# A tree-attention kernel: each iteration's Q/K transposes move ahead of its score matmuls, and the K copy moves ahead of its exponentials

## The chip, the cores and the metric

One NeuronCore of a Trainium2 chip runs the whole program. The metric is the device time in microseconds of one execution. Five executions of the kernel before were timed, and one further execution was taken by the hardware profiler; the profile's own span runs from the program's first to its last instruction, and the execution's time is a little longer than that span.

## The reference

Attention over 8 batches of 12 heads, 512 positions and 64 dimensions, where position i sees only itself and its ancestors in a binary tree (parent of i is (i-1)//2):

```python
mask = np.zeros((seq, seq))
for i in range(seq):
    mask[i, i] = 1
    parent = i
    while parent > 0:
        parent = (parent - 1) // 2
        mask[i, parent] = 1
scores = np.einsum('bhqd,bhkd->bhqk', Q, K) * scale
scores = scores + (1 - mask) * (-1e9)
weights = np.exp(scores - np.max(scores, axis=-1, keepdims=True))
weights = weights / (np.sum(weights, axis=-1, keepdims=True) + 1e-10)
return np.einsum('bhqk,bhkd->bhqd', weights, V).astype(np.float32)
```

## The kernel before

The unit of work is a pair of heads: 8 batches of 6 pairs make 48 pairs, numbered 0 to 47. Since a position has few ancestors, a pair doesn't compute the full 512x512 score matrix. It scores every query against one tile of 128 keys near the root (`st1`, two heads of 128x512) and against four further tiles of 128 keys, each for 96 queries (`stx`, two heads of 128x384). The mask is put into PSUM by a matmul of constant codes (`ctile`) before the matmul of K and Q adds the scores.

A pair passes through three functions.

- `transposes(i)` (line 267): 16 TensorE transposes, 8 of Q into the PSUM tile `tq` and 8 of K into `tk`; then VectorE copies `tq` to the SBUF tile `qt` (line 297), and ScalarE copies `tk` to `kt` (line 298).
- `scores(i)` (line 304): TensorE writes the codes and then K times Q into `st` (one copy in PSUM), ScalarE takes the exponential into `et` (line 324); then TensorE does the same for `stx` (one copy), and ScalarE takes the exponential into `etx` (line 335).
- `values(i)` (line 342): 48 TensorE matmuls of `et` and `etx` with V and a column of ones into `o` (one copy in PSUM); VectorE takes the reciprocal of the sums (line 364) and multiplies (line 367); SyncE issues the output DMA of 256 KB (line 371).

`tq`, `tk`, `st`, `stx` and `o` stand in PSUM pools with one buffer each, so the next pair's writer waits until the last pair's reader is done. `qt` and `kt` have four buffers, `et` and `etx` three.

The inputs come in by DMAs that GpSimd issues (line 222), which turn fp32 into bf16 on the way. A hand-written plan sets their order. For a batch b between 1 and 6 it is: Q and K of heads 0 to 3, Q and K of heads 4 to 7, V of batch b+1, Q and K of heads 8 to 11. GpSimd does nothing else and runs ahead of the compute. V has to be spread into two layouts by VectorE: `copies(spread(...))` (line 261) gives ten copies for each batch, two in each of the iterations of pairs 1 to 5 of the batch before. The last batch has no such copies, since no V is left.

The whole program runs under a manual schedule, so that each engine executes its instructions in program order. The loop is a software pipeline:

```python
for i in range(N):
    b, hp = pairs[i]
    load(i + 9)
    if i + 1 < N:
        scores(i + 1)
    if i + 2 < N:
        transposes(i + 2)
    values(i)
```

TensorE's order in iteration i is therefore scores of i+1, transposes of i+2, values of i. ScalarE's order is exponential of `st` and of `stx` of pair i+1, then the K copy of pair i+2. VectorE's order is the Q copy of i+2, the reciprocal and the product of i, then the V copies.

Of the kernel before, what the change touches and what calls it, by code (L numbers as in the profile page):

```python
# [126 lines left out]
def kernel(  # L127
# [88 lines left out]
    def load(upto):  # L216
        while plan and plan[-1][0] <= upto:
            _, src, b, h0, h1 = plan.pop()
            kind = "q" if src is Q else "k" if src is K else "v"
            if (kind, b) not in loaded:  # L220
                loaded[kind, b] = stage.tile([P, H, T * D], bf16, name=kind + "s")
            nc.gpsimd.dma_start(  # L222
                out=loaded[kind, b][:, h0:h1, :],
                in_=src[b, h0:h1].rearrange("h (p t) d -> p h (t d)", t=T),
            )
# [6 lines left out]
    def spread(b, h0, h1):  # L232
        vs = loaded["v", b]
        v1, vx = v1s[b % NV], vxs[b % NV]
        v = vs[:, h0:h1, :].rearrange("p h (t d) -> p h t d", t=T)
        big = [
            (vx[64:P, h0:h1, 0:3:2, 0:D], v[64:P, :, 0:3:2, :]),
            (vx[0:64, h0:h1, 1:4:2, 0:D], v[64:P, :, 1:4:2, :]),
        ]
        for part, c, t0, t1 in ((0, 0, 1, 2), (32, 0, 3, 0), (64, 1, 2, 1),  # L240
                                (96, 1, 0, 3)):
            assert KORD[XW[c] + part // 32] == (t0, 1)
            assert KORD[XW[c + 2] + part // 32] == (t1, 1)
            big.append((
                vx[part:part + 32, h0:h1, c:c + 3:2, 0:D],
                pick(v[32:64], t0, t1),
            ))
        small = [
            (v1[32 * r:32 * r + 32, h0:h1, 0:D], v[0:32, :, KORD[K1 + r][0], :])
            for r in range(T)  # L250
        ]
        ops = []
        for n in range(6):
            ops.append(big[n])
            if n % 3:
                ops.append(small.pop())
        return ops

    def copies(ops):
        for o, i in ops:  # L260
            nc.vector.tensor_copy(out=o, in_=i)  # L261

    pairs = [(b, hp) for b in range(B) for hp in range(HP)]
    N = len(pairs)
    state = {}

    def transposes(i):
        b, hp = pairs[i]
        qs, ks = loaded["q", b], loaded["k", b]
        tq = psumT.tile([P, 512], bf16)  # L270
        tk = psumT.tile([P, 576], bf16)

        def put(o, src, t, mat):
            for hi in range(2):
                nc.tensor.matmul(  # L275
                    out=o[D * hi:D * hi + D], rhs=perms[mat],
                    lhsT=src[:, 2 * hp + hi, D * t:D * t + D],
                    start=True, stop=True, is_transpose=True,
                )

        put(tq[:, 64:192], qs, 0, 1)
        put(tq[:, 0:384].rearrange("d (c x) -> d c x", c=2)[:, :, 0:64], qs, 1, 0)
        for t in range(2, T):
            put(tq[:, P * t:P * t + P], qs, t, 0)
        for t in range(T):
            at = kput[t][1]
            if at[1] - at[0] == 32:
                step, run = at[2] - at[0], 64
            else:
                step, run = at[1] - at[0], 32  # L290
                assert at[2] - at[1] == step
            o = tk[:, at[0]:]
            o = bass.AP(o.tensor, o.offset, [list(o.ap[0]), [step, P // run], [1, run]])
            put(o, ks, t, 2 + t)
        qt = work.tile([P, 512], bf16)
        kt = work.tile([P, 512], bf16)
        nc.vector.tensor_copy(out=qt[:, :], in_=tq[:, :])  # L297
        nc.scalar.copy(  # L298
            out=kt[:, :].rearrange("d (i j x) -> d i j x", j=2, x=32),
            in_=tk[:, :].rearrange("d (j i x) -> d i j x", j=2, x=32)[:, 0:8],  # L300
        )
        state[i] = (qt, kt)

    def scores(i):
        b, hp = pairs[i]
        q_, k_ = state[i]
        st1 = psumS.tile([P, 2, 512], fp32)
        stx = psumS.tile([P, 2, 512], fp32)

        def mm(dst, lhsT, rhs, first):  # L310
            nc.tensor.matmul(  # L311
                out=dst, lhsT=lhsT, rhs=rhs, start=first, stop=True,
                skip_group_check=not first,
            )

        hb = [slice(D * hi, D * hi + D) for hi in range(2)]
        q = [q_[hb[hi], :] for hi in range(2)]
        k = [k_[hb[hi], :] for hi in range(2)]
        for hi in range(2):
            mm(st1[:, hi, :], ck1[hb[hi], :], cq1[hb[hi], :], True)  # L320
        for hi in range(2):
            mm(st1[:, hi, :], k[hi][:, 32 * K1:32 * K1 + P], q[hi], False)
        et1 = et1pool.tile([P, 2, 512], bf16)
        nc.scalar.activation(  # L324
            out=et1[:, :, :], in_=st1[:, :, :], func=AF.Exp, scale=scale
        )
        for hi in range(2):
            mm(stx[:, hi, 0:384], ckx[hb[hi], :], cqx[hb[hi], :], True)
        for c in range(T):
            for hi in range(2):  # L330
                mm(stx[:, hi, 96 * c:96 * c + 96],
                   k[hi][:, 32 * XW[c]:32 * XW[c] + P],
                   q[hi][:, P * c + 32:P * c + P], False)
        etx = etxs[i % NX]
        nc.scalar.activation(  # L335
            out=etx[:, :, :, 32:P],
            in_=stx[:, :, 0:384].rearrange("p h (c q) -> p h c q", c=T),
            func=AF.Exp, scale=scale,
        )
        state[i] = (et1, etx)  # L340

    def values(i):
        b, hp = pairs[i]
        v1, vx = v1s[b % NV], vxs[b % NV]
        et1, etx = state.pop(i)
        o2 = psumO.tile([P, 2, 512], fp32)
        for hi, order in ((0, (0, 1)), (1, (0, 1)), (0, (2, 3)), (1, (2, 3))):
            h = 2 * hp + hi
            for t in order:
                for kind in range(2):  # L350
                    parts = ((0, P, t),) if t >= 2 else (
                        (0, 64, 1 - t), (64, P, t))
                    for p0, p1, c in parts:
                        if kind == 0:
                            e, v = et1[:, hi, P * c + p0:P * c + p1], v1[:, h, 0:D + 1]
                        else:
                            e, v = etx[:, hi, c, p0:p1], vx[:, h, c, 0:D + 1]
                        nc.tensor.matmul(  # L358
                            out=o2[p0:p1, hi, (D + 1) * t:(D + 1) * (t + 1)],
                            lhsT=e, rhs=v, start=kind == 0, stop=kind == 1,  # L360
                        )
        o4 = o2[:, :, 0:T * (D + 1)].rearrange("p h (t x) -> p h t x", t=T)
        rec = opool.tile([P, 2, T, 1], fp32)
        nc.vector.reciprocal(out=rec[:, :, :, :], in_=o4[:, :, :, D:D + 1])  # L364
        of = opool.tile([P, 2, T * D], fp32)
        of4 = of[:, :, :].rearrange("p h (t d) -> p h t d", t=T)
        nc.vector.tensor_tensor(  # L367
            out=of4, in0=o4[:, :, :, 0:D],
            in1=rec[:, :, :, :].to_broadcast([P, 2, T, D]), op=ALU.mult,
        )  # L370
        nc.sync.dma_start(
            out=out[b, 2 * hp:2 * hp + 2].rearrange(
                "h (p t) d -> p h (t d)", t=T
            ),
            in_=of[:, :, :],
        )

    E = mybir.EngineType
    with tc.manual_schedule(engines={E.PE, E.DVE, E.Activation, E.Pool}):
        load(3)  # L380
        transposes(0)
        scores(0)
        transposes(1)
        copies(spread(0, 0, 6))
        for i in range(N):
            b, hp = pairs[i]
            load(i + 9)
            if i + 1 < N:
                scores(i + 1)
            if i + 2 < N:  # L390
                transposes(i + 2)
            values(i)
            if b == 0:
                if hp in (0, 3):
                    todo = spread(0, 6, H) if hp == 0 else spread(1, 0, H)
                cuts = (0, 3, 6, 10)
                copies(todo[cuts[hp % 3]:cuts[hp % 3 + 1]])
            elif b + 1 < B and hp:
                if hp == 1:
                    todo = spread(b + 1, 0, H)  # L400
                copies(todo[2 * hp - 2:2 * hp])
# [30 lines left out]
```

## Time and profile before

| what | value |
|---|---|
| five timed executions | 157.3, 157.62, 158.47, 159.35 and 160.69 us, median 158.47 us |
| the profiled execution's own time | 158.21 us, with a span of 156.4 us |
| mean granted TensorE clock in it | 0.957 |
| busy: TensorE matmul, ScalarE, VectorE, GpSimd | 114.1, 107.5, 104.7, 48.4 us |
| packets of the input queue | 37840, 18.88 MB |
| packets of the output and constants queue | 13344, 13.08 MB |

In the lines of the profile, PE is TensorE's matmul, PEld its weight load, DVE is VectorE, ACT is ScalarE, POOL is GpSimd and SP is SyncE; L298 is line 298 of the kernel, and `kt<-tk` says that the instruction writes `kt` from `tk`. Times are in microseconds from the span's start unless they are marked ns. A bracket at the end of a line gives how long the engine sat idle before it, and what ended the wait.

### The profile page before, as it was taken

How to read it: one execution, taken by the hardware profiler on the slowest of the kernel's cores; microseconds unless marked ns; L12 is line 12 of the kernel's file. 1: busy time of each engine (PE TensorE's matmuls, PEld its weight loads, DVE VectorE, ACT ScalarE, POOL GpSimd, SP SyncE). 2: the span in 40 equal slices, each digit the busy share in tenths (PEclk: the TensorE clock that was granted, in tenths of full speed). 3: DMA queues.
4: the chain of work that ended last, by engine and by line, in shares of the span. 5: the costliest groups of instructions: out<-in, count | busy, mean ns of one | idle time of the engine just before them, and what ended most of it. 6: DMA issues, size and time to landing. Idle time of an engine off the chain costs nothing.

```text
span 156.4 us, 5916 instructions
## 1 busy us (share of the span) xinstructions
PE 114.1 (73%) x2592; PEld 79.9 (51%) x2592; DVE 104.7 (67%) x243; ACT 107.5 (69%) x145; POOL 48.4 (31%) x65
## 2 busy tenths in 40 slices
PE   0427967848598878787887848978787887878750
PEld 0213845635465556465564625756464655646440
DVE  2107898987269768885878564795888678774531
ACT  3143878866557878778787874878788787878840
POOL 7954623321444133403332034503341130000000
PEclk9999999999659999999999996899999999999995
DMA  5999999999999999999999999999999999953232
GB/s 140 134 182 195 183 218 227 227 236 221 230 211 223 234 231 228 237 226 236 225 234 233 227 237 221 218 225 231 234 227 239 226 234 229 242 157 116 97 109 93
DMA packets 51211, 32.33 MB, mean 207 GB/s; under 512 B 1777, under 2 KB 51057, under 8 KB 51185
## 3 DMA queue, kind: packets, MB, share of 16 engines
q0 software_dynamic: 37840, 18.88, 89.5%
q1 hardware_dynamic: 13344, 13.08, 29.5%
q8 instruction: 20, 0.33, 0.8%
q14 instruction: 7, 0.05, 0.1%
HBM read 38.24 MB, written 12.58 MB: 325 GB/s over the span
## 4 chain that ended last, share of the span: by engine, by line
DMA 56%; ACT 18%; issue 10%; PE 9%; POOL 3%; DVE 1%; ACTq 0%; POOLq 0%
DMA ks<-in_K_dram 23%; DMA qs<-in_Q_dram 19%; DMA vs<-in_V_dram 14%; ACT etx L335 9%; PE st L311 6%; ACT kt L298 6%; ACT et L324 3%; PE o L358 2%; POOL vs L222 1%; POOL qs L222 1%; POOL ks L222 1%; DVE of L367 1%; PE stx L311 1%; PE tk L275 1%; PE tq L275 0%
## 5 line engine op out<-in xcount | busy, mean ns | idle before, releaser
L324 ACT ACTIVATE et<-st 128x1024 bf16<-128x1024 f32 x48 | 49.2, 1024 | 30.8 <-PE st L311 30.8
L311 PEld LDWEIGHTS <-kt 64*128 64x128 bf16 x480 | 19.3, 98 | 42.9 <-ACT kt L298 32.5
L358 PE MATMUL o<-v,et 128*64 128x65 bf16 (+1 forms) x576 | 36.7, 199 | 3.4 <-DVE v L261 2.3
L335 ACT ACTIVATE etx<-stx 128x768 bf16<-128x768 f32 x48 | 38.6, 804 | 0.0
L358 PE MATMUL o<-vx,etx 128*64 128x65 bf16 (+1 forms) x576 | 36.6, 197 | 0.0
L298 ACT COPY kt<-tk 128x512 bf16<-128x512 bf16 x48 | 28.4, 591 | 11.8 <-PE tk L275 11.8
L311 PE MATMUL st<-qt,kt 64*128 64x512 bf16 x96 | 19.9, 410 | 20.6 <-ACT kt L298 19.1
L367 DVE TENSOR_TENSOR of<-o,rec 128x512 f32<-128x512 f32 x48 | 33.2, 691 | 1.7
L297 DVE COPY qt<-tq 128x512 bf16<-128x512 bf16 x48 | 20.2, 421 | 20.5 <-PE tq L275 19.5
L222 POOL DMA_DIRECT2D qs<-in_Q_dram x26 | 19.9, 765 | 44.9 <-DMA vs<-in_V_dram 29.4
L358 PEld LDWEIGHTS <-et 128*64 128x64 bf16 (+1 forms) x576 | 29.4, 109 | 6.0 <-DVE v L261 2.6
L261 DVE COPY vx<-vs 32x1536 bf16<-32x1536 bf16 (+3 forms) x54 | 29.1, 539 | 1.2
L358 PEld LDWEIGHTS <-etx 128*64 128x64 bf16 (+1 forms) x576 | 29.1, 109 | 0.0
L222 POOL DMA_DIRECT2D ks<-in_K_dram x26 | 19.7, 759 | 27.9 <-DMA qs<-in_Q_dram 19.6
L275 PE MATMUL tq<-ptile,qs 128*64 128x128 bf16 x384 | 21.0, 234 | 9.1 <-DMA qs<-in_Q_dram 9.1
L364 DVE RECIPROCAL rec<-o 128x8 f32<-128x8 f32 x48 | 9.9, 207 | 23.4 <-PE o L358 23.4
L275 PE MATMUL tk<-ptile,ks 128*64 128x128 bf16 x384 | 20.3, 231 | 4.7 <-DMA ks<-in_K_dram 4.7
L311 PE MATMUL st<-ctile 64*128 64x512 bf16 x96 | 19.8, 409 | 0.0
L275 PEld LDWEIGHTS <-qs 128*64 128x64 bf16 x384 | 12.9, 114 | 13.2 <-DMA qs<-in_Q_dram 9.6
L275 PEld LDWEIGHTS <-ks 128*64 128x64 bf16 x384 | 14.4, 117 | 5.8 <-DMA ks<-in_K_dram 5.7
L311 PE MATMUL stx<-qt,kt 64*128 64x96 bf16 x384 | 16.8, 209 | 0.0
L311 PE MATMUL stx<-ctile 64*128 64x384 bf16 x96 | 16.6, 342 | 0.0
(11 smaller groups left out, 33.8 us busy)
## 6 DMA issues: line engine op xcount, KB each, us to landing
out_dram<-of SPq DMA_DIRECT2D x48, 256.0 KB, 6.3
qs<-in_Q_dram POOLq DMA_DIRECT2D x22, 256.0 KB, 18.8
ks<-in_K_dram POOLq DMA_DIRECT2D x22, 256.0 KB, 18.6
vs<-in_V_dram POOLq DMA_DIRECT2D x7, 768.0 KB, 22.3
vs<-in_V_dram POOLq DMA_DIRECT2D x2, 384.0 KB, 8.8
qs<-in_Q_dram POOLq DMA_DIRECT2D x4, 128.0 KB, 11.9
ks<-in_K_dram POOLq DMA_DIRECT2D x4, 128.0 KB, 11.9
ctile<-tree_codes SPq DMA_DIRECT2D x1, 288.0 KB, 2.8
```

What stands on the lines that cost most here:

```text
L222: nc.gpsimd.dma_start(out=loaded[kind, b][:, h0:h1, :], in_=src[b, h0:h1].rearrange("h (p t) d -> p h (t d)", t=T),)
L261: nc.vector.tensor_copy(out=o, in_=i)
L275: nc.tensor.matmul(out=o[D * hi:D * hi + D], rhs=perms[mat], lhsT=src[:, 2 * hp + hi, D * t:D * t + D], start=True, stop=True, is_transpos ...
L297: nc.vector.tensor_copy(out=qt[:, :], in_=tq[:, :])
L298: nc.scalar.copy(out=kt[:, :].rearrange("d (i j x) -> d i j x", j=2, x=32), in_=tk[:, :].rearrange("d (j i x) -> d i j x", j=2, x=32)[:, 0:8],
L311: nc.tensor.matmul(out=dst, lhsT=lhsT, rhs=rhs, start=first, stop=True, skip_group_check=not first,)
L324: nc.scalar.activation(out=et1[:, :, :], in_=st1[:, :, :], func=AF.Exp, scale=scale)
L335: nc.scalar.activation(out=etx[:, :, :, 32:P], in_=stx[:, :, 0:384].rearrange("p h (c q) -> p h c q", c=T), func=AF.Exp, scale=scale,)
L358: nc.tensor.matmul(out=o2[p0:p1, hi, (D + 1) * t:(D + 1) * (t + 1)], lhsT=e, rhs=v, start=kind == 0, stop=kind == 1,)
L364: nc.vector.reciprocal(out=rec[:, :, :, :], in_=o4[:, :, :, D:D + 1])
L367: nc.vector.tensor_tensor(out=of4, in0=o4[:, :, :, 0:D], in1=rec[:, :, :, :].to_broadcast([P, 2, T, D]), op=ALU.mult,)
```

## The change

In the loop, `transposes(i + 2)` is called before `scores(i + 1)`. With the manual schedule this changes the order on two engines. TensorE now executes transposes of i+2, scores of i+1, values of i. ScalarE now executes the K copy of i+2, the exponential of `st` of i+1, the exponential of `stx` of i+1. VectorE's order and the order of the DMAs stay as they were, and no instruction is added or removed.

```diff
             load(i + 9)
+            if i + 2 < N:
+                transposes(i + 2)
             if i + 1 < N:
                 scores(i + 1)
-            if i + 2 < N:
-                transposes(i + 2)
             values(i)
```

## The prediction

> **What bounds the kernel now.** I write T(n), S(n) and V(n) for the TensorE parts of transposes, scores and values of pair n. First the page's slices, by tenth of busy time, for the whole run:
>
> ```profile
> span 156.4 us, 5916 instructions
> ...
> PEclk9999999999659999999999996899999999999995
> DMA  5999999999999999999999999999999999953232
> ```
>
> The DMA engines are full from the second slice to about 137 us, the end of the loads. TensorE's clock falls twice. Next the waits, because busy shares of some 70% say that a chain and not one engine holds the compute:
>
> ```profile
> PEld L311 <- ACT kt L298: 32.5, 40, 0.8
> ACT et L324 <- PE st L311: 30.8, 48, 1.8
> ...
> PE st L311 <- ACT kt L298: 19.1, 36, 0.5
> ...
> PE tk L275 <- DMA ks<-in_K_dram: 4.7, 5, 2.0
> ```
>
> TensorE's score matmul waits for ScalarE's K copy, and ScalarE's first exponential waits for that matmul: a ring. ScalarE's timeline gives its length:
>
> ```profile
> 124.39 1.02 ACT L324 ACTIVATE et<-st 128x1024 bf16<-128x1024 f32 x1 [0.55 <-PE st L311]
> 125.31 0.80 ACT L335 ACTIVATE etx<-stx 128x768 bf16<-128x768 f32 x1
> 126.00 0.59 ACT L298 COPY kt<-tk 128x512 bf16<-128x512 bf16 x1
> 127.14 1.02 ACT L324 ACTIVATE et<-st 128x1024 bf16<-128x1024 f32 x1 [0.55 <-PE st L311]
> ```
>
> From start to start 0.92 + 0.69 + 0.65 (copy and handover) + 0.49 (matmul to exponential) = 2.75 us, in nearly every iteration: 16.5 us for the six pairs of a batch. But look where TensorE meets the K load of heads 8 to 11 in batches 4 and 6 (pairs 28 and 40), in the timeline:
>
> ```profile
> 94.46 0.41 PE L275 MATMUL tk<-ptile,ks 128*64 128x128 bf16 x8 [2.00 <-DMA ks<-in_K_dram]
> ...
> 127.30 0.41 PE L275 MATMUL tq<-ptile,qs 128*64 128x128 bf16 x8
> ...
> 127.67 0.41 PE L275 MATMUL tk<-ptile,ks 128*64 128x128 bf16 x8
> ```
>
> T(28) waited 2.00 us, and T(40) began its K half 0.37 us after its Q half instead of the usual 0.25: that load had landed 0.04 us before. In batches 3 and 5 the trace has the same load landing 0.26 and 0.58 us before its use. So the ring and the loads run neck and neck up to 127.67 us. The DMA view, for 12 to 16 us (loads alone) and 100 to 132 us (both), prices the loads:
>
> ```profile
> q0 software_dynamic: 1565, 0.78, 145.0%
> ...
> q0 software_dynamic: 8439, 4.21, 96.7%
> q1 hardware_dynamic: 3212, 3.11, 35.8%
> ```
>
> Alone, 4 us / 1565 = 2.56 ns of all engines for a load packet. In the mixed stretch 8439 x 2.56 = 21.6 us, so the 3212 output packets took 10.4 us, 3.2 ns each. Output packets are 13344 less 288 of the constants over 48 pairs, 272 each, hence 0.87 us. A batch needs 37840/8 x 2.56 + 6 x 0.87 = 17.3 us of DMA. This is more than 16.5. From the landing for T(16) at 57.32 to that for T(40) at 127.63 the trace has 70.3 us, 17.6 a batch. **The loads bind until T(40); only what follows is bound by the ring.**
>
> **What the Trainium skill says.** "DMA: Bandwidth & Descriptors", section "Issuing engines are not separate DMA queues": DMAs of all issuers share 16 engines and interleave. The trace agrees (the two queues fill one budget above), so an output that is made earlier delays a load. "TensorE: Matmul & The Clock Gate", section "What's actually happening": after an idle window of about 3.4 us TensorE's clock is halved until a busy window. The trace agrees on the length: half speed at 40.57 to 47.39 and 95.18 to 98.59 us, 6.83 and 3.41 us. The same page's "Why this matters for your kernels" warns of idle gaps above some 3 us; here the 2.00 us gap before 94.46 sufficed, and I follow the trace. The section "Architectural detail: the array is 16× 32×32, not 1× 128×128" has ScalarE and VectorE as strict first-in-first-out queues; the trace agrees, no instruction overtakes a waiting one on them.
>
> **The change, part by part.** Nothing is added; two orders are swapped.
>
> *The ring is cut.* The copy of K for pair i+2 now runs before the exponentials of i+1, and S(i+2) comes an iteration later, so the copy no longer stands between S and the exponential. ScalarE's own sum is 0.92 + 0.69 + 0.49 = 2.10 us (the last is my value for a copy followed at once by an exponential, 0.59 less the 0.10 by which its other neighbours overlap; never seen here, 0.45 to 0.60). TensorE's own sum, from starts at full clock: S from 17.30, T from 18.17, V from 18.64 to the next S at 19.33, so S 0.87 (half for `st`, half for `stx`), T 0.47, V 0.70, together 2.04. VectorE becomes the longest where V copies run:
>
> ```profile
> 128.73 0.21 DVE L364 RECIPROCAL rec<-o 128x8 f32<-128x8 f32 x1 [0.47 <-PE o L358]
> 128.97 0.69 DVE L367 TENSOR_TENSOR of<-o,rec 128x512 f32<-128x512 f32 x1
> 129.69 0.35 DVE L261 COPY v<-vs 32x768 bf16<-32x768 bf16 x1
> 130.06 0.55 DVE L261 COPY vx<-vs 32x1536 bf16<-32x1536 bf16 x1
> 130.53 0.41 DVE L297 COPY qt<-tq 128x512 bf16<-128x512 bf16 x1
> ```
>
> From the reciprocal to the end of the Q copy 2.21, with the next start 2.25 us. So a batch of compute takes about 13 us, and 14 to 16 with a half-speed window: below 17.3. *Up to T(40) the gain is zero:* TensorE reaches T(40) early and stands.
>
> *The new wait.* T(40) now stands ahead of S(39) and V(38), which queue behind it on TensorE; behind those wait ScalarE's exponentials and VectorE's product. Before, S(39) had passed. V(37) ends about 13 to 14.3 us after T(34)'s K at 111, so TensorE idles about 3 us but for the Q half.
>
> *From T(40) to the end,* from the K half's start at zero. T 0.22, S(39) to 1.09, V(38) from 1.09 to 1.79. The reciprocal follows a V's start by 0.84 (111.22 to 112.08 before, rounded down): 1.93; product, copies and Q copy of T(41) end at 4.15. T(42) needs that copy because `tq` has one buffer: 4.21. T(43), T(44), T(45) follow VectorE, 2.25 each: 6.46, 8.71, 10.96. The iterations after 41 have no copies, so T(46) follows TensorE at 13.0 and T(47) ScalarE at 15.1. S(47) waits for the exponential of pair 46 to free `st` (ends 17.4) and `stx` (18.1): it ends at 18.6. V(46) runs to 19.3; reciprocal and product end at 20.4; V(47) starts at 20.5. In the trace of before V(47) starts at 151.22 and the span ends at 156.35, 5.13 later. **Sum 25.6 us.** Before, from 127.67 to 156.35, it was 28.7. Gain 3.1. Pair 42's K needs about 3.6 us of DMA after pair 40's (1056 packets and one output), T(42) asks at 4.2; later loads are further ahead. So no load binds again.
>
> *Given back.* (1) Outputs leave earlier. Where T(40) stands, up to two more pairs' outputs have been written (36 were by 127.63, by the count of packets), 0 to 1.7 us; VectorE's products before T(40) end only about 1 us earlier than now, so I take half a pair, 0.5. (2) The idle 3 us halves the clock. At half clock before, S began at 95.55, T at 97.15, V at 98.00, the next S at 98.94: 3.4 an iteration. One window of 3.4 us loses 1.7 us of TensorE work, of which about 0.5 was slack under VectorE: 1.2. No window costs 0; two, as at 40.57, where the next window was partly idle too, 3.4.
>
> Net 3.1 - 0.5 - 1.2 = 1.4 us off the profiled 158.21: **156.8 us**. That time is 0.26 below the median, which is within the spread of the five runs.
>
> **The rivals.**
> - *No half-speed window, or outputs that cost nothing.* For: the window's phase is free, and a stall split over two windows may pass (34 to 36 us before, no drop). Against: twice out of two gaps like this one it fell. 158.2 - 3.1 + 0.3 = 155.4.
> - *Nothing left.* Two full outputs ahead of the load (1.7) and one window: 158.2 - 3.1 + 1.7 + 1.2 = 158.0. For: the queue drains while TensorE stands. Against: outputs took 6 us to land.
> - *Slower: the stalled TensorE comes back at half clock for two windows.* T(40) holds S(39) and V(38) behind it, the window that contains the landing is under three quarters busy as that of 40.6 to 44 was, and the half clock goes on into S(40) to V(40): 158.2 - 3.1 + 0.5 + 3.4 = 159.0; with both outputs 160.2. It decides from about 2.6 us of lost TensorE time on.
> - *The ring was the bound throughout.* 2.75 to 2.2 in 48 iterations, 26 us off, 132. The packet budget excludes it: 37840 x 2.56 + 44 x 0.87 = 135 us before the last load even lands.
>
> **How the numbers follow.** Forecast case 0.46, no half-speed window 0.26, nothing left 0.13, slower 0.13, the ring throughout 0.02. A measurement of this kernel can tell about 1% from no change, so faster means below 156.9. The forecast lies on that edge: a little less than half of it is faster, nearly all of the second case and the last; slower starts at 160.1, which takes half of the slower case and some 0.04 for what the trace does not show; the rest is within 1%. This gives 0.48, 0.41, 0.11. The range goes from no window and no delay with 0.8 us of spread between runs (154.4) to two windows with most of an output more (159.6).
>
> **What would show it.** In the changed profile: the exponential of `st` no longer idles 0.55 us behind TensorE in stretches without loads due; steps of 2.25 us in iterations with V copies and 2.1 in the last batch; TensorE waits of 2 us and more for K loads in every batch from the third; T(40)'s K half at 128.1 us, give or take 0.7; half clock right after it; 25.6 to 27 us from there to the end. A K half of T(40) well before 127 us would prove the packet budget wrong; steps of 2.4 us or more in the last batch would prove the cut of the ring wrong.

## The result, and the profile after

The changed kernel takes 157.2 us (median of 40 runs) against 158.64 us (median of 75 runs) of the kernel before: a ratio of 0.988, with a 95% interval of 0.985 to 0.991. The ratio leaves out executions that took over 1.5% longer than the fastest of their kernel and the medians don't, so the medians alone give 0.991. The profiled execution took 156.98 us with a span of 155.1, against 158.21 and 156.4 before. The forecast was 156.8 us. I read the profile after in the order of the prediction. The page first:

```profile
span 155.1 us, 5918 instructions
...
PEclk9999999599999995699999999999659999999998
DMA  5999999999999999999999999999999999963432
```

The DMA engines are full over the same stretch as before. The clock now falls three times ahead of the end instead of twice. The waits:

```profile
ACT kt L298 <- PE tk L275: 34.4, 28, 5.3
...
PE tq L275 <- DMA qs<-in_Q_dram: 13.1, 5, 5.8
...
PE tk L275 <- DMA ks<-in_K_dram: 7.5, 6, 2.0
...
ACT et L324 <- PE st L311: 3.1, 7, 0.7
...
PEld L311 <- ACT kt L298: 0.6, 1, 0.6
```

The ring is gone: ScalarE's exponential waits 3.1 us for the score matmul instead of 30.8, and the score matmul's weight load waits 0.6 us for the K copy instead of 32.5. The idle time stands elsewhere. ScalarE's K copy waits 34.4 us for its transposes, and TensorE's K transposes wait 7.5 us for loads instead of 4.7. Part of what the ring no longer takes, the loads take: TensorE's waits for loads, Q and K together, grow from 13.8 to 20.6 us, and ScalarE's K copy stands behind them. ScalarE's timeline near the end shows what has replaced the ring:

```profile
143.17 0.59 ACT L298 COPY kt<-tk 128x512 bf16<-128x512 bf16 x1
143.72 1.02 ACT L324 ACTIVATE et<-st 128x1024 bf16<-128x1024 f32 x1
144.64 0.81 ACT L335 ACTIVATE etx<-stx 128x768 bf16<-128x768 f32 x1
145.33 0.59 ACT L298 COPY kt<-tk 128x512 bf16<-128x512 bf16 x1
```

No line has a bracket: ScalarE runs without a gap, 0.55 + 0.92 + 0.69 = 2.16 us from copy to copy. Here is where pairs 34 and 40 meet their loads, in TensorE's timeline:

```profile
109.38 0.61 PE L275 MATMUL tq<-ptile,qs 128*64 128x128 bf16 x8 [2.03 <-DMA qs<-in_Q_dram]
...
111.55 0.64 PE L275 MATMUL tk<-ptile,ks 128*64 128x128 bf16 x8 [1.56 <-DMA ks<-in_K_dram]
...
127.21 0.41 PE L275 MATMUL tq<-ptile,qs 128*64 128x128 bf16 x8
...
127.45 0.39 PE L275 MATMUL tk<-ptile,ks 128*64 128x128 bf16 x8
```

T(34) stood for its loads, T(40) didn't: its K had landed at 126.95, half a microsecond earlier. The windows view says why TensorE came no earlier. Its columns are the stretch and its length, the busy time and instructions of TensorE's matmuls, its weight loads, VectorE, ScalarE and GpSimd, then the granted TensorE clock, the DMA share and GB/s:

```profile
109.50:116.20 6.70, 5.14 (x72) 3.32 (x72) 1.59 (x4) 2.55 (x4) 2.96 (x4) 0.50 1.36 225
127.50:130.90 3.40, 3.23 (x74) 2.27 (x70) 3.21 (x8) 3.15 (x5) 0.46 (x1) 1.00 1.31 233
```

The half clock came with T(34)'s Q half, at 109.45 us, for two windows of 3.41 us, and not after T(40). From the K half of T(40) to the end it is 27.65 us (127.45 to 155.1), where before it was 28.7.

### The profile page after: what moved, and what is told of

Same layout as the page of the kernel before. It is cut to its first block, busy times and chain, and to the rows that moved or that the text cites. A ratio compares the mean times of both kernels' runs of the same rounds, so it can differ in the third digit from the quotient of the medians.

```text
span 155.1 us, 5918 instructions
## 1 busy us (share of the span) xinstructions
PE 117.6 (76%) x2592; PEld 84.9 (55%) x2592; DVE 102.9 (66%) x243; ACT 110.2 (71%) x145; POOL 48.2 (31%) x65
## 4 chain that ended last, share of the span: by engine, by line
DMA 68%; PE 13%; DVE 8%; issue 4%; ACT 3%; POOL 2%; POOLq 0%
DMA ks<-in_K_dram 25%; DMA qs<-in_Q_dram 22%; DMA vs<-in_V_dram 20%; PE o L358 5%; DVE of L367 3%; PE st L311 2%; DVE vx L261 2%; PE stx L311 2%; PE tq L275 2%; ACT etx L335 2%; PE tk L275 2%; POOL qs L222 1%; DVE rec L364 1%; DVE v L261 1%; POOL ks L222 1%
## 5 line engine op out<-in xcount | busy, mean ns | idle before, releaser
L298 ACT COPY kt<-tk 128x512 bf16<-128x512 bf16 x48 | 28.2, 587 | 34.9 <-PE tk L275 34.4
L358 PE MATMUL o<-v,et 128*64 128x65 bf16 (+1 forms) x576 | 38.2, 203 | 6.2 <-DVE v L261 4.9
L358 PE MATMUL o<-vx,etx 128*64 128x65 bf16 (+1 forms) x576 | 37.2, 198 | 0.1
L358 PEld LDWEIGHTS <-et 128*64 128x64 bf16 (+1 forms) x576 | 28.3, 109 | 13.0 <-DVE v L261 6.1
L222 POOL DMA_DIRECT2D qs<-in_Q_dram x26 | 19.7, 758 | 43.0 <-DMA vs<-in_V_dram 26.9
L261 DVE COPY vx<-vs 32x1536 bf16<-32x1536 bf16 (+3 forms) x54 | 28.7, 532 | 1.2
L275 PE MATMUL tk<-ptile,ks 128*64 128x128 bf16 x384 | 21.7, 235 | 8.8 <-DMA ks<-in_K_dram 7.5
L275 PEld LDWEIGHTS <-qs 128*64 128x64 bf16 x384 | 15.0, 115 | 20.2 <-DMA qs<-in_Q_dram 13.7
L275 PEld LDWEIGHTS <-ks 128*64 128x64 bf16 x384 | 15.4, 119 | 10.4 <-DMA ks<-in_K_dram 8.8
L311 PEld LDWEIGHTS <-ctile 64*128 64x128 bf16 x192 | 10.7, 97 | 11.9 <-issue 3.2
```

Of the source, the lines that this page charges most:

```text
L222: nc.gpsimd.dma_start(out=loaded[kind, b][:, h0:h1, :], in_=src[b, h0:h1].rearrange("h (p t) d -> p h (t d)", t=T),)
L275: nc.tensor.matmul(out=o[D * hi:D * hi + D], rhs=perms[mat], lhsT=src[:, 2 * hp + hi, D * t:D * t + D], start=True, stop=True, is_transpos ...
L298: nc.scalar.copy(out=kt[:, :].rearrange("d (i j x) -> d i j x", j=2, x=32), in_=tk[:, :].rearrange("d (j i x) -> d i j x", j=2, x=32)[:, 0:8],
L311: nc.tensor.matmul(out=dst, lhsT=lhsT, rhs=rhs, start=first, stop=True, skip_group_check=not first,)
L358: nc.tensor.matmul(out=o2[p0:p1, hi, (D + 1) * t:(D + 1) * (t + 1)], lhsT=e, rhs=v, start=kind == 0, stop=kind == 1,)
```

## The experiments

### The new order early or late only

The diff is against the changed kernel.

```diff
-            if i + 2 < N:
+            if i >= 38 and i + 2 < N:      # late_only; i < 38 in early_only
                 transposes(i + 2)
             if i + 1 < N:
                 scores(i + 1)
+            if not (i >= 38) and i + 2 < N:
+                transposes(i + 2)
             values(i)
```

> The new order holds only from iteration 38 (the transposes of pair 40) on; iterations 0 to 37 keep the old one. Theory (loads bind until the transposes of pair 40, the ring only after it): the whole gain is kept, a ratio to before of 0.980 to 0.991, with the K half of pair 40's transposes at 127 to 128.5 us as in both kernels. Rival (every iteration is a little shorter, the gain is spread over the run): only 10 of 48 iterations have it, so 0.997.

> The new order holds only in iterations 0 to 37; from the transposes of pair 40 on the old order. Theory (loads bind until there): no gain, a ratio of 0.995 to 1.005. Rival (the gain is spread over the run): 38 of 48 iterations have it, so 0.990.

The late order gave 0.989 (0.986 to 0.993), the early one 0.999 (0.996 to 1.002). So the last ten iterations bring the whole gain, as far as these intervals can tell, and 38 of 48 iterations bring nothing that can be told from zero. The rival of a gain spread over the run is out, since 0.997 and 0.990 lie outside the two intervals. In the profile with the late order, K of pair 40 was reached at 126.52 us, a little earlier than the 127 to 128.5 expected.

### Without most of the loads

The same edit was made in the kernel before and in the changed kernel.

```diff
+    plan = [x for x in plan if x[2] < 2]
     plan.reverse()
...
-        qs, ks = loaded["q", b], loaded["k", b]
+        qs, ks = loaded["q", b % 2], loaded["k", b % 2]
...
-        vs = loaded["v", b]
+        vs = loaded["v", b % 2]
```

> The kernel before, but only the inputs of batches 0 and 1 are loaded, and the later batches compute on them again (so the loads of batches 2 to 7 are left out); all compute and all outputs stay. Theory (without loads the ring of 2.75 us alone is left): the K of pairs 10 and 11 lands at about 37 us, then 37 iterations of 2.75 us to the transposes of pair 47 and 9.8 us to the end: 150 us, range 147 to 152. Rival (loads don't bind before, the ring binds from the start): 155 or more.

> The changed kernel with the same loads left out. Theory (the cut of the ring is worth 0.5 us an iteration wherever no load binds): 37 iterations of about 2.3 us from 37 us on and 10.5 us to the end: 134 us, range 128 to 138, steps of 2.25 us with V copies and 2.1 without, TensorE's clock full. Rival (the new order is bound by an engine or by the clock at nearly the old pace): 147 or more.

The old order took 152.3 us, a ratio of 0.961 (0.954 to 0.968) to the kernel before, the new one 139.9 us, a ratio of 0.882 (0.875 to 0.888). Take the loads away and the same change is worth 12.35 us instead of 1.44. Both kernels took longer than their ranges allowed, the old order by 0.3 and the new one by 1.9 us: T(10) was at 39.3 and 39.9 us instead of 37, and the new order's 37 steps were 2.38 us on the mean instead of 2.3. ScalarE's timeline, old order and then new:

```profile
110.60 1.02 ACT L325 ACTIVATE et<-st 128x1024 bf16<-128x1024 f32 x1 [0.55 <-PE st L312]
...
113.35 1.02 ACT L325 ACTIVATE et<-st 128x1024 bf16<-128x1024 f32 x1 [0.55 <-PE st L312]
```

```profile
112.23 0.59 ACT L299 COPY kt<-tk 128x512 bf16<-128x512 bf16 x1
112.78 1.02 ACT L325 ACTIVATE et<-st 128x1024 bf16<-128x1024 f32 x1
113.70 0.81 ACT L336 ACTIVATE etx<-stx 128x768 bf16<-128x768 f32 x1
114.76 0.59 ACT L299 COPY kt<-tk 128x512 bf16<-128x512 bf16 x1 [0.26 <-PE tk L276]
115.37 1.02 ACT L325 ACTIVATE et<-st 128x1024 bf16<-128x1024 f32 x1
```

The old ring is 2.75 us in every step. In the new order one copy starts 0.55 us ahead of the exponential, and the next first waits 0.26 us for its transposes. Over a batch the six steps between transposes are 2.16, 2.58, 2.16, 2.50, 2.24 and 2.68 us, together 14.3 instead of 16.5. That is what the cut is worth where nothing else binds: 2.2 us a batch.

### TensorE's order alone

In the changed kernel, the K copy is taken out of `transposes` and made a function `copy_k` of its own (its lines, and the two calls ahead of the loop, are left out of the diff).

```diff
             if i + 2 < N:
                 transposes(i + 2)      # without the K copy
             if i + 1 < N:
                 scores(i + 1)
+            if i + 2 < N:
+                copy_k(i + 2)          # ScalarE, behind the exponentials
             values(i)
```

> TensorE has the new order, but ScalarE copies K behind the two exponentials as before. Theory (the ring is cut only if the copy leaves its place between exponential and matmul): the ring stays, and now the transposes stand in it too, because the scores of i+2 queue behind the transposes of i+3, which wait for the same copy to free the PSUM tile: 2.75 + 0.57 = 3.3 us a step. This is slower than the loads, so it binds from about pair 10 on: 40 + 37 x 3.3 + 10.5 us, a ratio of about 1.10 (1.06 to 1.13). Rival (TensorE's order alone brings the gain, the copy's place is of no account): 0.98 to 1.00.

It took 177.1 us in both of its two executions, a ratio of 1.116 (1.109 to 1.123), within what was expected. ScalarE's timeline:

```profile
99.28 1.02 ACT L329 ACTIVATE et<-st 128x1024 bf16<-128x1024 f32 x1 [1.10 <-PE st L316]
100.20 0.80 ACT L340 ACTIVATE etx<-stx 128x768 bf16<-128x768 f32 x1
100.90 0.59 ACT L304 COPY kt<-tk 128x512 bf16<-128x512 bf16 x1
102.59 1.02 ACT L329 ACTIVATE et<-st 128x1024 bf16<-128x1024 f32 x1 [1.10 <-PE st L316]
```

The step is 3.31 us, and the exponential's wait has doubled from 0.55 to 1.10, since transposes now stand between copy and scores. So moving TensorE's transposes alone doesn't cut the ring but lengthens it; the cut takes the copy's new place on ScalarE as well. Moving the copy alone was not tried, so whether it would do by itself stays open.

### Keeping the clock across the stall

The order is that of the late kernel above; its part of the diff is left out here.

```diff
+        if i == 37:                     # in values, behind its matmuls
+            for n in range(23):
+                nc.tensor.matmul(
+                    out=o2[:, n % 2, 264:488], lhsT=ctile[:, 0:128],
+                    rhs=ctile[:, 128:352], start=True, stop=True)
```

> The kernel with the new order from iteration 38 on, and 23 matmuls of constants into unused columns of PSUM (some 2.2 us of TensorE) behind the values of pair 37, so that TensorE does not stand idle ahead of pair 40's transposes. Theory (the idle time halves the clock and this costs about 1.1 us): full clock after the transposes of pair 40, the step from pair 40 to 41 is 2.6 instead of 3.5 us, a ratio to before of 0.980 to 0.986 against 0.989 without them. Rival (the slow first step is that of the work queued behind the wait, not of the clock): 0.989 or more.

The ratio is 0.986 (0.981 to 0.991), against 0.989 (0.986 to 0.993) without these matmuls: the intervals overlap, so the time alone settles nothing. The traces do. The windows right after T(40), with the late order alone and then kept warm:

```profile
126.90:130.30 3.40, 3.40 (x54) 2.38 (x54) 0.57 (x2) 2.31 (x3) 0.57 (x1) 0.50 1.31 238
```

```profile
128.00:131.40 3.40, 3.40 (x78) 2.45 (x80) 2.90 (x7) 2.91 (x5) 0.71 (x1) 1.00 1.42 205
```

TensorE was busy throughout both, and did 54 matmuls at half clock and 78 at full clock. From the K half of T(40) to that of T(41) it took 3.50 us (126.52 to 130.02) against 2.18 (127.98 to 130.16), and to the end 27.8 against 26.9 us. By these two executions, a stall that halves the clock costs about 0.9 us here. The matmuls of constants have a price of their own: pair 37's reciprocal, which must wait for them, began at 127.01 instead of 124.10 us. The Trainium skill ("TensorE: Matmul & The Clock Gate", section "Terms") puts the penalty at the throttled time times the share of the clock taken away, 1.7 us for a window of 3.41; the measured cost is about half of that. That the other engines' share of the steps covers the rest is my reading and wasn't tried by itself.

### The landing of K put forward

```diff
-            plan += [(at + 3, V, b + 1, 0, H), (at + 4, Q, b, 8, H),
-                     (at + 4, K, b, 8, H)]
+            plan += [(at + 3, Q, b, 8, H), (at + 3, K, b, 8, H),
+                     (at + 4, V, b + 1, 0, H)]
...
-            elif b + 1 < B and hp:
+            elif b + 1 < B and hp >= 3:  # ten copies as 4, 3, 3
```

> The changed kernel, with V of batch b+1 loaded behind instead of ahead of Q and K of heads 8 to 11 of batch b (b from 1 to 6), and its ten copies in the iterations of pairs 3, 4 and 5 (4, 3 and 3). Theory (the K load of heads 8 to 11 binds): that load lands some 3.9 us earlier (1536 packets of 2.56 ns), the transposes of pair 40 come 2 to 3.9 us earlier, up to 0.8 us of it is lost again to the crowded copies: a ratio to before of 0.963 to 0.980. Rival (what comes after is bound by the engines and not by when this load lands): 0.988, or worse by the crowded copies.

The ratio is 0.984 (0.977 to 0.991): not as good as expected, and not to be told from the changed kernel's 0.988. My expectation left out what comes next. The K load of pair 40 did land earlier, at 121.01 us instead of 126.95. But V now stands ahead of the next batch, and in the timeline the next load is the one that holds:

```profile
124.88 0.39 PE L275 MATMUL tk<-ptile,ks 128*64 128x128 bf16 x8
...
130.45 0.41 PE L275 MATMUL tq<-ptile,qs 128*64 128x128 bf16 x8 [1.10 <-DMA qs<-in_Q_dram]
...
132.43 0.41 PE L275 MATMUL tk<-ptile,ks 128*64 128x128 bf16 x8 [1.56 <-DMA ks<-in_K_dram]
```

T(40) came 2.6 us earlier than in the changed kernel (124.88 against 127.45), and T(42) came at 132.43 against 132.26. What stands in the queue ahead of pair 42 is the same in either order. Here an exchange of places within the full queue moved the wait and did not remove it.

### VectorE's V copies in the tail

```diff
-            elif b + 1 < B and hp:
+            elif b + 1 < B - 1 and hp:   # no_last_v_copies
```

```diff
         for o, i in ops:
-            nc.vector.tensor_copy(out=o, in_=i)
+            small = len(o.shape) == 3
+            (nc.gpsimd if b == 6 and small else nc.vector).tensor_copy(out=o, in_=i)
```

The second diff is gpsimd_takes_small_copies on the changed kernel, and late_warm_gpsimd on the one kept warm.

> The changed kernel without VectorE's ten V copies for batch 7 (left out, so the values of the last batch are computed on older V). Theory (in the tail TensorE waits for VectorE's copies in every second iteration, and the first values of batch 7 wait for the last copy): the steps from pair 40 to 47 become 2.16 us each, 15.1 us together instead of 16.5 to 17.4, a ratio to before of 0.974 to 0.984. Rival (TensorE's own work and the landing of the loads set the tail): 0.988 as the changed kernel.

> The changed kernel, with the four small V copies of batch 7 (32x768) on GpSimd, behind its last load issue at about 128 us, instead of on VectorE. Theory (in the tail VectorE's V copies cost TensorE time in every second step, and the values of pair 42 wait for the last of them): up to 0.4 us in each of two or three steps, tail from pair 40's K half 0.5 to 1 us shorter than in the changed kernel unless GpSimd's own copies end after 138 us; a ratio to before of 0.980 to 0.986. Rival (GpSimd's copies slow VectorE's down, or are late for pair 42): 0.990 or more.

> The new order from iteration 38 on, the matmuls of constants behind pair 37's values that keep the clock, and the four small V copies of batch 7 on GpSimd. Theory: the two savings add, about 0.9 us for the clock and 0.5 us for the copies, on top of the order's 1.7: a ratio to before of 0.976 to 0.984, the best of all so far. Rival (they hide the same wait): 0.984 to 0.989.

Without the last V copies the ratio is 0.983 (0.976 to 0.989), and from the K half of T(40) to that of T(47) it takes 16.2 us instead of 17.4. The first three steps are 2.2 to 2.3 us, near the 2.16 expected; two later ones are 2.6, so the sum isn't 15.1. Both of these hold a gap in which TensorE waited for nothing that the profile shows (0.21 and 0.26 us), like the gap in T(44) of the changed kernel that is read further down. The ratio alone can't be told from the changed kernel's 0.988. With the small copies on GpSimd the ratio is 0.990 (0.978 to 1.001), too wide to say anything; its profile has steps of 2.16 us from T(42) on but for one of 2.37. With both savings it is 0.995 (0.991 to 0.998), outside what either the theory or its rival gave. I don't read this as worse than the changed kernel: its median is 157.06 us, against 158.7 for the kernel before timed beside it, and the changed kernel's is 157.2. But the expected saving isn't there. The timeline of that last kernel, GpSimd and VectorE, shows one reason:

```profile
128.44 3.89 POOL L262 COPY v<-vs 32x768 bf16<-32x768 bf16 x4
```

```profile
129.48 2.17 DVE L262 COPY vx<-vs 64x1536 bf16<-64x1536 bf16 x2
```

Two VectorE copies of 64x1536 took 2.17 us while GpSimd copied, and 1.13 and 1.12 us at the same place in the kernels before and after. T(41)'s Q transposes had to wait 1.4 us for the Q copy that stands behind these copies on VectorE. The matmuls of constants also held up pair 37's reciprocal, to 128.51 us, as they write the same PSUM tile. So VectorE's copies cost tail time, about 1.2 us by the traces of one execution each, but GpSimd was no cheap place for them. No version that I ran is shown to be faster than the changed kernel.

## Why the prediction was right

**The bound.** That the loads hold until about T(40) and the ring only behind it is shown from both sides: by the late and early orders (0.989 and 0.999), and by leaving loads out, which makes the gain some nine times as large. In the profiled execution T(40) itself just escaped its load; the last load that held TensorE was T(34)'s.

**The ring.** Its cut is shown, and so is that TensorE's half of the change can't do it without the copy's move (1.116).

**T(40)'s place.** I gave 128.1 us, give or take 0.7, for its K half; it was 127.45. The place is right and the reasoning behind it was not: I let TensorE stand about 3 us ahead of T(40). It stood 3.6 us ahead of T(34) instead, came back at half clock for two windows, needed 15.7 us from its K half to the Q half of T(40), and met a load that had landed half a microsecond before. Nor did TensorE wait 2 us for a K load in every batch from the third: T(16) waited 2.00, T(28) 1.76 and T(34) 1.56 us, T(22) and T(40) not at all.

**The half clock.** I subtracted 1.2 us for one window behind T(40). The profiled execution had none there. With the late order it was there and cost about 0.9 us, by one execution against one of the kernel kept warm. So the term was of about the right size, but this execution had its half clock elsewhere, at T(34). The stall that I put at 34 to 36 us in the kernel before, without a drop, was TensorE's from 32.9 to 34.6 us.

**From T(40) to the end.** I worked out 25.6 us without half clock; it was 27.65. The part from T(47)'s K half on was right: 10.3 us by my steps, 10.3 measured. The miss is in the seven steps before, 15.3 us by my steps and 17.4 measured. The kernel with two batches of loads, at full clock, took 16.5 for the same seven. So 1.2 us were mis-sized: ScalarE's copy to exponential takes 0.55 and not 0.49 us, which makes the step 2.16 and not 2.10; where V copies run, steps of 2.16 and some 2.5 alternate, where I had 2.25; and the first values of a batch wait for the last V copy, which I had left out. The other 0.9 us are of this execution, in the step from T(43) to T(44), 3.09 us against 2.24 with two batches of loads. The timeline:

```profile
135.67 0.33 PE L275 MATMUL tk<-ptile,ks 128*64 128x128 bf16 x5 [0.73 <-issue]
...
139.56 0.22 PE L358 MATMUL o<-v,et 128*64 128x65 bf16 x2 [0.53 <-DVE v L261]
```

The second line is the wait of V(42) for the last V copy, one of the mis-sized parts. The first is a gap inside T(44) in which TensorE waited for nothing that the profile shows. The traces point to a cause: TensorE waited for its own instructions. A pair has 54 matmuls (24 of them in `values`, not 48) and as many weight loads, so the run has 5184. The DMA view lists 20 transfers of 16 KB on queue 8, of the kind instruction, about one for each 256 of them. In the traces of all runs there are 11 gaps of over 0.15 us in which TensorE did nothing and waited for nothing shown. Each comes at the same place of a block of 256, with the DMA engines full and the new order in force, 1.3 to 1.6 us after such a transfer ended. Neither kernel with two batches of loads has one. No run tests this cause by itself.

**Outputs.** I took 0.5 us for outputs that are written ahead of the K load of pair 40. That load landed at 126.95 us after and 127.63 before, so no cost is seen. The term had the wrong sign in this execution: by the count of packets 35 outputs had been written by then, against 36 before, probably because TensorE's earlier stalls had held the compute back. One output at 0.87 us is near the 0.68 us by which the load came earlier.

In sum: 3.1 - 0.5 - 1.2 = 1.4 us was forecast. The spans differ by 1.2 us, 1.0 of it behind the K half of T(40) and 0.2 ahead of it. The mechanism is right, but that the total fits so closely is luck, because two errors cancel: a tail that was sized 2.05 us too short, and deductions of 1.7 us that this execution didn't pay at that place. It ran the course of my first rival, with no half clock behind T(40) and outputs that cost nothing, and still took 156.98 and not 155.4 us.

## What to carry to other kernels

When a ring of waits and a full DMA queue run at nearly the same pace, count the packets ahead of each late load before valuing a faster ring: the ring's gain counts only behind the last load that the compute waits for, here 10 of 48 iterations. In an in-order pipeline, look for what stands between a copy and the work behind it on both engines; moving one engine's order alone made the ring longer. Before shifting places within a full queue, look at the next load: here the wait moved to it.

## What was not expected of the hardware

- After the first 15 us, each of the seven stops of TensorE of 2.0 us and more in these traces was followed by half clock, for one or two windows of 3.41 us. Shorter stops could go either way: with the late order, 0.93 us ahead of T(40)'s Q half and 1.11 us ahead of its K half were followed by it, and without the last V copies 1.55 us ahead of that K half were not.
- Two VectorE copies of 64x1536 bf16 took 2.17 instead of 1.13 us while GpSimd ran its own copies; one of 32x1536 in another kernel, also during GpSimd's copies, took its usual 0.55 us.
- GpSimd took 3.7 to 3.9 us for four copies of 32x768, which take VectorE 0.35 us each.
- With the loads' DMA traffic beside them, transfers of TensorE's own instructions seem to have come late enough to stop it for up to 0.73 us; the kernels without these loads show no such gap.
